# First MLP product as seven block products instead of eight, with its activations kept in DRAM

## The chip, the cores and the metric

The kernel runs on one core of a Trainium2 chip. The metric is device time in microseconds. A profile of one execution gives, for each engine (PE for matrix products, DVE for vector work, ACT for activations and copies, SP for issuing DMAs), when each instruction ran and what released it.

## The reference, cut to what matters

One layer of a diffusion block over 1024 latent tokens with 1024 features. Everything up to the MLP (norm, input projection, RG-LRU, Fourier mixing, merge, output projection) is the same before and after. The part that changes:

```python
def sq_relu_mlp(h, w1, w2):
    return jnp.square(jax.nn.relu(h @ w1)) @ w2

x = x + gt2 * sq_relu_mlp(modulate(rms_norm(x, g_mlp[i]), sh2, sc2), w1[i], w2[i])
return rms_norm(x, g_final)
```

Here `h` is 1024 tokens x 1024 features, `w1` is 1024 x 4096 and `w2` is 4096 x 1024, all in float32.

## The kernel before

Every float32 product is carried by three passes over an exact split x = hi + lo into the float32r type: hi\*hi + hi\*lo + lo\*hi. A split (`split`, L84) is a copy to hi on ACT and a subtraction to lo on DVE. A matmul instruction takes a 128 x 128 weight block and 512 columns.

Activations lie feature-major. Weights of `w1` come as 32 blocks of 128 output features; one block holds 8 slices of 128 input features. `Stream` (L94) loads such blocks three ahead into the four `wr` buffers (`wr_tile`, L78) and splits them two ahead into `wh` and `wl` (three buffers each).

Before the MLP, `out_mm` (L815) makes the output projection in two halves of 512 features (`dh`), eight token tiles each; a finished tile is added to `x2`, normalised by `norm_tile` (L795) into `xn`, and `norm_half` (L801) transposes four token tiles at a time, modulates them (scale and shift, on ACT or DVE) and splits them into `h2[h]`.

The MLP runs in eight chunks (`c`, L904) of four blocks (`f`). For each block `ff1` (L864) makes 2 token halves x 8 slices x 3 passes = 48 matmuls into a PSUM tile, `act` (L870) applies relu, squares and splits the result, and `load_w2` (L879) loads, scales by the gate and splits the matching rows of `w2`. Then `ff2` (L884) multiplies the chunk for eight token tiles, and DVE adds each result to `x2[i]` (L936). The products of one chunk and the vector work of the next overlap. After the last chunk the rows are normalised and stored.

What sets the order: outside of one early block, a planner orders the instructions of each engine by priority and by when it thinks that inputs are ready; `tc.high_priority(offset=...)` raises a priority by so many instructions. Inside `tc.manual_schedule` the instructions of the named engines keep the written order among themselves. All DMAs go through SP's one queue. Buffers come from tagged pools: `pg` has 24 of 1024 columns, `yp` 17, `wr` four; PSUM has three tiles of two banks (`mm_ps`) and two of one bank (`sm_ps`).

Of the kernel before, what the change touches and what calls it, by code (L numbers as in the profile page):

```python
"""Hybrid RG-LRU / Fourier diffusion block on one NeuronCore.

Activations are kept feature-major ([feature, token]); every float32 matrix product is
carried by three float32r passes over an exact split x = hi + lo (hi = float32r(x),
lo = x - hi, both exact in float32r): hi*hi + hi*lo + lo*hi.
"""
# [39 lines left out]
def f32(ap):  # L46
    return ap.bitcast(F32)
# [3 lines left out]
def block_kernel(es: ExitStack, tc: tile.TileContext, a, out):  # L51
# [13 lines left out]
    def nm(s):  # L65
        uid[0] += 1
        return f"{s}_{uid[0]}"
# [7 lines left out]
    def sm_ps():  # L75
        return psum.tile([P, HB], F32, tag="sm", name=nm("smp"), bufs=2)
# [17 lines left out]
    class Stream:  # L94
        """weight pages in the order of use: loads run three ahead, splits two ahead"""

# [38 lines left out]
    order += [(a["wlo"][m], W8) for m in range(KT)]  # L135
    order += [(a["w1"][f], W8) for f in range(FF // P)]
    weights = Stream(order)
# [3 lines left out]

# [1 line left out]
    ident = const.tile([P, P], F32, name="ident")  # L143
# [65 lines left out]
    gt_d = dram.tile([2, D], F32, name="gt_d")  # L209
    gyb_d = dram.tile([KT, P, T], F32, name="gyb_d")  # L210

    # persistent, small
    mod = const.tile([P, 64], F32, name="mod")
# [10 lines left out]
    def gemv_acc(wm, which, acc=None, ks=range(KT)):  # L224
        """silu(c) @ w_mod by rows, shift and scale of a pair of feature tiles"""
        if acc is None:
            acc = gacc[:, 4 * P * (nacc[0] % 2):4 * P * (nacc[0] % 2 + 1)]
            nacc[0] += 1
        for k in ks:
            sc = col(8 * which + k, silu)  # L230
            w = wm[k // 2][:, k % 2, :]
            if k == 0:
                V.tensor_scalar(acc, w, sc, None, ALU.mult)
            else:
                V.scalar_tensor_tensor(acc, w, sc, acc, ALU.mult, ALU.add)
        return acc

    def gemv_cols(kp, which, acc, ps=None):
        """columns of shift and (1 + scale) * g"""
        ps = sm_ps() if ps is None else ps  # L240
        for j in range(4):
            PE.matmul(ps[:, j:j + 1], acc[:, P * j:P * (j + 1)], ones, start=True, stop=True)
        b, kt = (M_SH1, M_SHC)[which] + 2 * kp, 2 * kp
        d = mod[:, b + 8:b + 10]
        V.tensor_tensor(mod[:, b:b + 2], ps[:, 0:4:2], pv[:, V_SH1 + kt:V_SH1 + kt + 2], ALU.add)
        V.tensor_tensor(d, ps[:, 1:4:2], pv[:, V_GMIX + kt:V_GMIX + kt + 2], ALU.mult)
        V.tensor_tensor(d, d, gb[:, kt:kt + 2], ALU.add)

    class Gemvs:
        """silu(c) @ w_mod for gates (rows, kept in DRAM) and the MLP's shift and scale, in steps"""  # L250

# [46 lines left out]

# [1 line left out]
    hT = [[page([P, T], F32R) for _ in range(2)] for _ in range(KT)]  # L300
# [16 lines left out]
    with tc.tile_pool(name="xp", bufs=16, reuse_waits="tile") as xp:  # L317
# [118 lines left out]

        # Fourier mixing, channels then positions, on the even/odd foldings of the inputs
        dcs = sm.tile([P, 130], F32, tag="dcs", name="dcs", bufs=1)
# [92 lines left out]
        ab += [page([P, 2, 2, NK], F32R) for _ in range(4)]  # L531
        # positions: rows are (group pair, channel frequency), columns the frequencies by parity
        pse = sm_ps()
# [35 lines left out]

# [1 line left out]
    prep_lam()  # L571
# [159 lines left out]

# [1 line left out]
    with tc.tile_pool(name="yp", bufs=17, reuse_waits="tile") as yp:  # L733
# [61 lines left out]
        def norm_tile(i):  # L795
            square_sum(x2[i], ss2[:, i:i + 1])
            r = rstd(ss2[:, i:i + 1])
            xn[i] = ypage([P, D])
            V.tensor_scalar(xn[i], x2[i], r, None, ALU.mult)

        def norm_half(h):  # L801
            for kt in range(KT):
                ps = sm_ps()
                for i in range(4):
                    PE.transpose(ps[:, i * P:(i + 1) * P], xn[4 * h + i][:, kt * P:(kt + 1) * P], ident)  # L805
                hf = sm.tile([P, HB], F32, tag="jk", name=nm("hf"), bufs=2)
                if kt % 2:
                    V.tensor_scalar(hf, ps, col(M_GS2 + kt, mod), col(M_SH2 + kt, mod), ALU.mult, ALU.add)
                else:
                    S.activation(hf, ps, AF.Identity, scale=col(M_GS2 + kt, mod), bias=col(M_SH2 + kt, mod))  # L810
                t = (page if h else ypage)([P, 2, HB], F32R)
                split(hf, t[:, 0], t[:, 1])
                h2[h][kt] = t

# [8 lines left out]
        for dh in range(2):  # L823
# [12 lines left out]
            for i in range(KT):  # L836
# [18 lines left out]
                if dh == 1:  # L855
                    norm_tile(i)
                    if i == 3:
                        norm_half(0)
        gv.reduce()
        norm_half(1)  # L860
        gt2 = const.tile([P, D], F32, tag="gt", name="gt2")
        dma(gt2, gt_d[1].partition_broadcast(P))

        def ff1(ps, w, h):  # L864
            for k in range(KT):
                for i, (l, r) in enumerate(passes(w, (h2[h][k][:, 0], h2[h][k][:, 1]))):
                    PE.matmul(ps[:, h * HB:(h + 1) * HB], l[:, k, :], r,  # L867
                              start=k == 0 and i == 0, stop=k == KT - 1 and i == 2)

        def act(ps):  # L870
            r = ypage([P, T])
            S.activation(r, ps, AF.Relu)
            hi, lo = ypage([P, T], F32R), ypage([P, T], F32R)
            S.activation(hi, r, AF.Square)  # L874
            V.tensor_tensor(r, r, r, ALU.mult)  # L875
            V.tensor_tensor(lo, r, f32(hi), ALU.subtract)
            return hi, lo
# [26 lines left out]
        for c in range(NC):  # L904
            av, wv = [], []
            if c == 0:
                ws, pss = [weights.take() for _ in range(3)], [mm_ps() for _ in range(3)]
                for h in range(2):
                    for w, ps in zip(ws, pss):
                        ff1(ps, w, h)  # L910
                for j, ps in enumerate(pss):
                    av.append(act(ps))
                    wv.append(load_w2(j))
            for f in range(len(av), CH):
                w, ps = weights.take(), mm_ps()
                for h in range(2):
                    ff1(ps, w, h)
                av.append(act(ps))
                wv.append(load_w2(c * CH + f))
            pss = [mm_ps() for _ in range(2)]  # L920
# [122 lines left out]
```

## Time and profile before

| what | value |
|---|---|
| runs shown, median (lowest to highest) | 1504.51 us (1504.46 to 1506.61) |
| span of the profiled execution, first to last instruction | 1501.4 us |
| PE busy | 1468.2 us, 98% of the span |
| DVE busy | 846.3 us, 56% |
| ACT busy | 536.6 us, 36% |
| DMA moved | 145.35 MB, mean 97 GB/s |

The page of the profile gives the execution's own time only as its span; a run's time has some 3 us beside it (1504.51 less 1501.4). Busy time counts the union of an engine's instructions; a matmul's shown duration overlaps the next one's, so what one costs is the distance between starts. In rows of instructions, "x24" means 24 merged ones, and a bracket gives the idle time before and what ended it.

### The profile page before, as it was taken

The numbers are of one execution on the slowest core, as the hardware profiler recorded it, in microseconds if no ns is written. First come the engines' busy times: TensorE is split into PE (matmuls) and PEld (weight loads), VectorE is DVE, ScalarE is ACT, GpSimd is POOL, SyncE is SP. The second block draws the span as 40 slices with busy tenths as digits, with TensorE's granted clock in tenths as the row PEclk, the third lists the DMA queues.
The fourth block names the chain that finished last, engine by engine and source line by source line (L and its number), as shares of the span: only waits on it lengthen the run. The fifth ranks groups of instructions, "written<-read, shape, count | busy, mean of one in ns | idle before, by whom it ended". The sixth has DMA issues, their size and how long they took to land.

```text
span 1501.4 us, 16062 instructions
## 1 busy us (share of the span) xinstructions
PE 1468.2 (98%) x6712; PEld 1193.8 (80%) x6712; DVE 846.3 (56%) x957; ACT 536.6 (36%) x643; POOL 0.7 (0%) x6
## 2 busy tenths in 40 slices
PE   5999999999999999999999999999999999999998
PEld 3888888878788877887778888888888888888886
DVE  7664649878987898556566343343424424343324
ACT  7443245765566647221254021120202113021122
POOL 0000000000000000000000000000000000000000
PEclk9999999999999999999999999999999999999999
DMA  8433612233313343559202020110202112020002
GB/s 329 175 112 119 237 39 81 101 124 133 110 61 128 115 150 126 182 177 339 73 29 98 14 85 28 56 56 28 72 14 71 42 43 66 5 85 28 28 1 112
DMA packets 42519, 145.35 MB, mean 97 GB/s; under 512 B 4755, under 2 KB 5163, under 8 KB 42447
## 3 DMA queue, kind: packets, MB, share of 16 engines
q1 hardware_dynamic: 42447, 144.34, 28.3%
q8 instruction: 52, 0.85, 0.2%
q14 instruction: 20, 0.16, 0.0%
HBM read 128.06 MB, written 16.26 MB: 96 GB/s over the span
## 4 chain that ended last, share of the span: by engine, by line
PE 89%; DVE 4%; DMA 2%; ACT 2%; issue 1%; SPq 0%; DVEq 0%; ACTq 0%
PE mm L867 24%; PE mm L889 23%; PE mm L307 23%; PE mm L819 6%; PE mm L762 5%; PE mm L607 2%; PE smp L582 2%; DMA wr<-in_win 1%; DVE l L639 1%; PE mm L483 1%; PE smp L608 1%; PE mm L672 1%; PE smp L805 1%; ACT jk L205 0%; DMA pg<-in_x 0%
## 5 line engine op out<-in xcount | busy, mean ns | idle before, releaser
L889 PE MATMUL mm<-pg,pg 128*128 128x512 f32 x1512 | 352.5, 394 | 0.0
L889 PEld LDWEIGHTS mm<-pg,pg 128*128 128x128 f32 x1512 | 283.8, 188 | 67.5
L867 PE MATMUL mm<-pg,wh 128*128 128x512 f32 x1024 | 323.1, 396 | 0.0
L307 PE MATMUL mm<-pg,wh 128*128 128x512 f32 x1120 | 308.7, 397 | 0.5 <-DVE pg L85 0.5
L307 PEld LDWEIGHTS mm<-pg,wh 128*128 128x128 f32 x1120 | 204.8, 189 | 43.8 <-DVE pg L85 1.0
L867 PEld LDWEIGHTS mm<-pg,wh 128*128 128x128 f32 x1024 | 191.9, 188 | 45.4
L85 ACT ACTIVATE wh<-wr 128x1024 fp32r<-128x1024 f32 (+2 forms) x92 | 91.3, 994 | 321.5 <-PE mm L867 161.1
L85 DVE TENSOR_TENSOR wl<-wr,wh 128x1024 fp32r<-128x1024 f32 (+2 forms) x92 | 104.8, 1141 | 172.9 <-ACT wh L85 172.9
L867 PE MATMUL mm<-pg,wl 128*128 128x512 f32 x512 | 201.8, 394 | 0.0
L85 ACT ACTIVATE pg<-wr 128x1024 fp32r<-128x1024 f32 (+1 forms) x55 | 51.2, 935 | 379.4 <-PE mm L889 262.6
L936 DVE TENSOR_TENSOR pg<-pg,mm 128x1024 f32<-128x1024 f32 x63 | 76.9, 1221 | 191.7 <-PE mm L889 191.7
L307 PE MATMUL mm<-pg,wl 128*128 128x512 f32 x560 | 175.4, 394 | 0.0
L307 PEld LDWEIGHTS mm<-pg,wl 128*128 128x128 f32 x560 | 105.4, 188 | 24.3
L867 PEld LDWEIGHTS mm<-pg,wl 128*128 128x128 f32 x512 | 96.2, 188 | 23.2
L819 PE MATMUL mm<-pg,pg 128*128 128x512 f32 x384 | 92.2, 397 | 0.1
L819 PEld LDWEIGHTS mm<-pg,pg 128*128 128x128 f32 x384 | 71.2, 188 | 18.2 <-DVE pg L85 1.2
L85 DVE TENSOR_TENSOR pg<-wr,pg 128x1024 fp32r<-128x1024 f32 (+1 forms) x55 | 58.3, 1067 | 25.9 <-ACT pg L85 25.9
L762 PE MATMUL mm<-pg,wh 128*128 128x512 f32 x256 | 70.1, 394 | 1.6 <-ACT pg L85 1.6
L875 DVE TENSOR_TENSOR pg<-pg 128x1024 f32<-128x1024 f32 x32 | 39.2, 1225 | 46.3 <-ACT pg L874 46.3
L762 PEld LDWEIGHTS mm<-pg,wh 128*128 128x128 f32 x256 | 47.9, 188 | 13.5 <-ACT pg L85 2.0
L205 ACT ACTIVATE jk<-pg 128x1024 bf16<-128x1024 f32 (+1 forms) x27 | 27.6, 1021 | 72.6 <-DVE pg L854 37.5
L747 DVE TENSOR_TENSOR wr<-wr,gt 128x1024 f32<-128x1024 f32 x32 | 39.2, 1225 | 24.4 <-DMA wr<-in_w 23.7
(216 smaller groups left out, 1496.3 us busy)
## 6 DMA issues: line engine op xcount, KB each, us to landing
wr<-in_w SPq DMA_DIRECT2D x64, 512.0 KB, 3.5
wr<-in_win SPq DMA_DIRECT2D x36, 512.0 KB, 4.5
pg<-in_wm SPq DMA_DIRECT2D x32, 512.0 KB, 7.8
wr<-in_wm SPq DMA_DIRECT2D x32, 512.0 KB, 3.7
pg<-in_x SPq DMA_DIRECT2D x16, 512.0 KB, 7.1
gyb_d<-l SPq DMA_DIRECT2D x8, 512.0 KB, 4.2
wr<-in_wlo SPq DMA_DIRECT2D x8, 512.0 KB, 4.3
wr<-ga_d SPq DMA_DIRECT2D x8, 512.0 KB, 4.2
```

What stands on the lines that cost most here:

```text
L85: return S.activation(hi, src, AF.Copy), V.tensor_tensor(lo, src, f32(hi), ALU.subtract)
L205: S.activation(j[:, 0:src.shape[1]], src, AF.Square, accum_out=dst)
L307: PE.matmul(ps[:, h * HB:(h + 1) * HB], l[:, k, :], r[:, h * HB:(h + 1) * HB], start=k == 0 and i == 0, stop=k == KT - 1 and i == 2)
L582: PE.matmul(pc[:, 0:TC], l[:, k, :], r[:, k % 4, :], start=k == 0 and i == 0, stop=k == KT - 1 and i == 2)
L607: PE.matmul(ps[:, h * HB:(h + 1) * HB], l, r[:, h * HB:(h + 1) * HB], start=i == 0, stop=i == 2)
L747: V.tensor_tensor(r, r, gate, ALU.mult)
L762: PE.matmul(ps[:, h * HB:(h + 1) * HB], l[:, k, :], r[:, h * HB:(h + 1) * HB], start=k == 0 and i == 0, stop=k == KT - 1 and i == 2)
L819: PE.matmul(ps, l, r, start=k == 0 and j == 0, stop=k == KT - 1 and j == 2)
L867: PE.matmul(ps[:, h * HB:(h + 1) * HB], l[:, k, :], r, start=k == 0 and i == 0, stop=k == KT - 1 and i == 2)
L875: V.tensor_tensor(r, r, r, ALU.mult)
L889: PE.matmul(ps[h], l, r[:, h * HB:(h + 1) * HB], start=f == 0 and j == 0, stop=f == CH - 1 and j == 2)
L936: V.tensor_tensor(x2[i], x2[i], pss[i], ALU.add)
```

## The change

The first MLP product, `w1` times `h`, is cut into 2 x 2 blocks: 16 pairs of feature blocks (a pair is 256 output features), two halves of the 1024 input features, two halves of the tokens. The block product is made by seven products with sums of blocks (Winograd's variant) instead of eight: with A the weights and B the activations, S1 to S4 are sums of weight blocks, T1 to T4 sums of activation blocks. Each product is 4 slices x 3 passes = 12 matmuls of 512 columns. Results that share terms are accumulated in the same PSUM bank, and DVE reads the bank between two products. The activations (relu, squared) are stored to `act_d` in DRAM, and `x2` to `x2_d`; both are loaded again for the second product. The two MLP products no longer alternate: first all 16 pairs, in a written order, then the eight chunks of `ff2`. The `Stream` no longer carries `w1`.

```diff
-    order += [(a["w1"][f], W8) for f in range(FF // P)]
...
+    x2_d = dram.tile([KT, P, D], F32, name="x2_d")
+    act_d = dram.tile([FF // P, P, T], F32, name="act_d")
...
+            dma(x2_d[i], x2[i])
+        def norm_block(kt, h, dst, on_vector):
+            ps = sm_ps()
+            for i in range(4):
+                PE.transpose(ps[:, i * P:(i + 1) * P], xn[4 * h + i][:, kt * P:(kt + 1) * P], ident)
+            if on_vector:
+                V.tensor_scalar(dst, ps, col(M_GS2 + kt, mod), col(M_SH2 + kt, mod), ALU.mult, ALU.add)
+            else:
+                S.activation(dst, ps, AF.Identity, scale=col(M_GS2 + kt, mod), bias=col(M_SH2 + kt, mod))
+        hf, tb = [], {n: [None] * 4 for n in ("b11", "b21", "b22", "t1", "t2", "t3", "t4")}
+        def norm_half0():
+            for k in range(4):
+                hf.append(page([P, 2, HB]))
+                for j in range(2):
+                    norm_block(k + 4 * j, 0, hf[k][:, j], j == 1)
+                    t = ypage([P, 2, HB], F32R)
+                    split(hf[k][:, j], t[:, 0], t[:, 1])
+                    tb[("b11", "b21")[j]][k] = (t[:, 0], t[:, 1])
+        def norm_half1(k):
+            g, t12, t34 = ypage([P, 2, HB]), *(wr_tile().rearrange("p (a b) -> p a b", b=HB) for _ in range(2))
+            for j in range(2):
+                norm_block(k + 4 * j, 1, g[:, j], False)
+            b11, b21, b12, b22 = hf[k][:, 0], hf[k][:, 1], g[:, 0], g[:, 1]
+            V.tensor_tensor(t12[:, 0], b12, b11, ALU.subtract)
+            V.tensor_tensor(t12[:, 1], b22, t12[:, 0], ALU.subtract)
+            V.tensor_tensor(t34[:, 0], b22, b12, ALU.subtract)
+            V.tensor_tensor(t34[:, 1], b21, t12[:, 1], ALU.subtract)
+            t = page([P, 2, HB], F32R)
+            split(b22, t[:, 0], t[:, 1])
+            tb["b22"][k] = (t[:, 0], t[:, 1])
+            for src, names in ((t12, ("t1", "t2")), (t34, ("t3", "t4"))):
+                hi, lo = page([P, 2, HB], F32R), page([P, 2, HB], F32R)
+                split(src, hi, lo)
+                for j, n in enumerate(names):
+                    tb[n][k] = (hi[:, j], lo[:, j])
...
-                        norm_half(0)
+                        norm_half0()
         gv.reduce()
-        norm_half(1)
...
+        class Pair:
+            def __init__(self, n):
+                self.n, self.w = n, {}
+            def load(self):
+                self.r = [wr_tile() for _ in range(2)]
+                for j, r in enumerate(self.r):
+                    dma(r, a["w1"][2 * self.n + j])
+            def put(self, src, names, hi, lo):
+                split(src, hi, lo)
+                for j, n in enumerate(names):
+                    self.w[n] = tuple(t[:, j * HB:(j + 1) * HB] for t in (hi, lo))
+            def hl(self, early=False):
+                if early:
+                    return ypage([P, 2 * HB], F32R), ypage([P, 2 * HB], F32R)
+                return tuple(wp.tile([P, 1024], F32R, tag=t, name=nm(t), bufs=3) for t in ("wh", "wl"))
+            def top(self, early=False):
+                self.put(self.r[0], ("a11", "a12"), *self.hl(early))
+            def sums13(self):
+                self.x = [ypage([P, 2 * HB]) for _ in range(2)]
+                (a11, a12), (a21, a22) = ([r[:, j * HB:(j + 1) * HB] for j in range(2)] for r in self.r)
+                self.q = a11, a12, a21, a22
+                V.tensor_tensor(self.x[0][:, 0:HB], a21, a22, ALU.add)
+                V.tensor_tensor(self.x[1][:, 0:HB], a11, a21, ALU.subtract)
+            def sums24(self):
+                a11, a12, a21, a22 = self.q
+                V.tensor_tensor(self.x[0][:, HB:], self.x[0][:, 0:HB], a11, ALU.subtract)
+                V.tensor_tensor(self.x[1][:, HB:], a12, self.x[0][:, HB:], ALU.subtract)
+            def s12(self):
+                self.put(self.x[0], ("s1", "s2"), *self.hl())
+            def s34(self):
+                self.put(self.x[1], ("s3", "s4"), *self.hl())
+            def last(self):
+                t = ypage([P, 2 * HB], F32R)
+                self.put(self.q[3], ("a22",), t[:, 0:HB], t[:, HB:])
+            def mm(self, ps, wn, tn, first):
+                for k in range(4):
+                    w = [t[:, k * P:(k + 1) * P] for t in self.w[wn]]
+                    for i, (l, r) in enumerate(passes(w, tb[tn][k])):
+                        PE.matmul(ps, l, r, start=first and k == 0 and i == 0, stop=k == 3 and i == 2,
+                                  skip_group_check=not first)
+            def p1(self):
+                ps = mm_ps()
+                self.A, self.B = ps[:, 0:HB], ps[:, HB:2 * HB]
+                self.e = (ypage if self.n else page)([P, 2 * HB])
+                self.mm(self.A, "a11", "b11", True)
+                S.activation(self.e[:, 0:HB], self.A, AF.Copy)
+            def p2(self):
+                self.f1 = page([P, T])
+                self.mm(self.A, "a12", "b21", False)
+                S.activation(self.f1[:, 0:HB], self.A, AF.Relu)
+            def p6(self):
+                self.mm(self.B, "s2", "t2", True)
+                V.tensor_tensor(self.e[:, HB:], self.e[:, 0:HB], self.B, ALU.add)
+            def p5(self):
+                self.C = sm_ps()
+                self.mm(self.C, "s1", "t1", True)
+            def p7(self):
+                self.f2 = page([P, T])
+                self.mm(self.B, "s3", "t3", False)
+                V.tensor_tensor(self.f2[:, HB:], self.e[:, 0:HB], self.B, ALU.add)
+                V.tensor_tensor(self.f2[:, HB:], self.f2[:, HB:], self.C, ALU.add)
+            def p3(self):
+                self.mm(self.C, "s4", "b22", False)
+                V.tensor_tensor(self.f1[:, HB:], self.e[:, HB:], self.C, ALU.add)
+                self.put_out(self.f1, 0)
+            def p4(self):
+                self.mm(self.B, "a22", "t4", False)
+            def out4(self):
+                V.tensor_tensor(self.f2[:, 0:HB], self.e[:, 0:HB], self.B, ALU.add)
+                self.put_out(self.f2, 1)
+            def put_out(self, t, j):
+                V.scalar_tensor_tensor(t, t, 0.0, t, ALU.max, ALU.mult)
+                dma(act_d[2 * self.n + j], t)
+        NP = FF // P // 2
+        pr = [Pair(n) for n in range(NP)]
+        with tc.high_priority(offset=PRIO):
+            pr[0].load()
+            pr[0].top()
+            pr[0].sums13()
+            pr[0].sums24()
+            pr[0].s12()
+            pr[0].s34()
+            pr[0].last()
+        with tc.manual_schedule(engines={mybir.EngineType.PE, mybir.EngineType.DVE, mybir.EngineType.Activation}):
+            pr[1].load()
+            pr[0].p1()
+            norm_half1(0)
+            pr[1].top(True)
+            pr[0].p2()
+            norm_half1(1)
+            pr[1].p1()
+            norm_half1(2)
+            pr[1].p2()
+            norm_half1(3)
+            pr[1].sums13()
+            pr[0].p6()
+            pr[1].sums24()
+            pr[1].s12()
+            pr[0].p5()
+            pr[2].load()
+            pr[0].p7()
+            pr[1].s34()
+            pr[1].last()
+            pr[0].p3()
+            pr[0].p4()
+            for n in range(1, NP):
+                c, nx = pr[n], pr[n + 1] if n + 1 < NP else None
+                if n > 1:
+                    c.p1()
+                pr[n - 1].out4()
+                if nx:
+                    nx.sums13()
+                c.p6()
+                if nx:
+                    nx.sums24()
+                c.p5()
+                if nx:
+                    nx.s12()
+                c.p7()
+                if n > 1:
+                    c.p2()
+                if nx:
+                    nx.top()
+                c.p3()
+                if nx:
+                    nx.s34()
+                    nx.last()
+                if n + 2 < NP:
+                    pr[n + 2].load()
+                c.p4()
+            pr[NP - 1].out4()
...
+        for i in range(KT):
+            x2[i] = page([P, D])
+            dma(x2[i], x2_d[i])
+        def load_act(f):
             hi, lo = ypage([P, T], F32R), ypage([P, T], F32R)
-            S.activation(hi, r, AF.Square)
-            V.tensor_tensor(r, r, r, ALU.mult)
-            V.tensor_tensor(lo, r, f32(hi), ALU.subtract)
+            load_split(act_d[f], hi, lo)
             return hi, lo
...
-            if c == 0:
-                ws, pss = [weights.take() for _ in range(3)], [mm_ps() for _ in range(3)]
-                for h in range(2):
-                    for w, ps in zip(ws, pss):
-                        ff1(ps, w, h)
-                for j, ps in enumerate(pss):
-                    av.append(act(ps))
-                    wv.append(load_w2(j))
-            for f in range(len(av), CH):
-                w, ps = weights.take(), mm_ps()
-                for h in range(2):
-                    ff1(ps, w, h)
-                av.append(act(ps))
-                wv.append(load_w2(c * CH + f))
+            for f in range(CH):
+                with tc.high_priority(offset=PRIO):
+                    av.append(load_act(c * CH + f))
+                    wv.append(load_w2(c * CH + f))
```

## Rows read from the trace of the kernel before

**Rows 1.** Page, parts 1 and 4: busy time, share, count; chain by engine and line.

```profile
PE 1468.2 (98%) x6712; PEld 1193.8 (80%) x6712; DVE 846.3 (56%) x957; ACT 536.6 (36%) x643; POOL 0.7 (0%) x6
...
PE mm L867 24%; PE mm L889 23%; PE mm L307 23%; PE mm L819 6%; PE mm L762 5%; PE mm L607 2%; PE smp L582 2%; DMA wr<-in_win 1%; DVE l L639 1%; PE mm L483 1%; PE smp L608 1%; PE mm L672 1%; PE smp L805 1%; ACT jk L205 0%; DMA pg<-in_x 0%
```

**Rows 2.** Stretches: us, busy PE, PEld, DVE, ACT, POOL, granted clock, DMA share, GB/s.

```profile
11.00:18.00 7.00, 2.00 (x5) 0.97 (x3) 6.79 (x15) 6.84 (x16) 0.00 (x0) 1.00 1.03 420
...
825.00:1450.00 625.00, 625.00 (x2689) 504.37 (x2688) 236.01 (x193) 112.77 (x110) 0.00 (x0) 1.00 0.14 43
```

**Rows 3.** Lines by form, 690 to 1500 us: count | busy us, mean ns | idle before.

```profile
L867 PE MATMUL mm<-pg,wh 128*128 128x512 f32 x1024 | 323.1, 396 | 0.0
L867 PE MATMUL mm<-pg,wl 128*128 128x512 f32 x512 | 201.8, 394 | 0.0
```

**Rows 4.** Same view, vector and activation forms that the new code uses.

```profile
L747 DVE TENSOR_TENSOR wr<-wr,gt 128x1024 f32<-128x1024 f32 x32 | 39.2, 1225 | 24.4 <-DMA wr<-in_w 23.7 <-DMA gt<-gt_d 0.2
L85 ACT ACTIVATE wh<-wr 128x1024 fp32r<-128x1024 f32 x29 | 30.8, 1060 | 161.1 <-PE mm L867 161.1
L853 DVE TENSOR_TENSOR g<-mm,gt 128x512 f32<-128x512 f32 x16 | 10.9, 687 | 22.5 <-PE mm L819 22.4
L898 DVE SCALAR_TENSOR_TENSOR pg<-pg,tiny,wr 128x1024 f32<-128x1024 f32 x7 | 9.0, 1284 | 0.2
L810 ACT ACTIVATE hf<-smp,mod 128x512 f32<-128x512 f32 x8 | 6.2, 777 | 3.4 <-PE smp L805 3.0 <-DVE pg L85 0.3
```

**Rows 5.** DVE in order of time: start, us; starts of neighbours show the pace.

```profile
710.16 1.29 DVE L853 TENSOR_TENSOR g<-mm,gt 128x512 f32<-128x512 f32 x2 [0.33 <-PE mm L819]
711.37 1.28 DVE L854 TENSOR_TENSOR pg<-pg,g 128x512 f32<-128x512 f32 x2
...
806.58 1.22 DVE L875 TENSOR_TENSOR pg<-pg 128x1024 f32<-128x1024 f32 x1
807.79 1.23 DVE L85 TENSOR_TENSOR pg<-wr,pg 128x1024 fp32r<-128x1024 f32 x1
808.93 1.22 DVE L876 TENSOR_TENSOR pg<-pg,pg 128x1024 fp32r<-128x1024 f32 x1
```

**Rows 6.** DVE in order of time, where the output projection ends.

```profile
776.42 1.42 DVE L799 TENSOR_SCALAR pg<-pg,tiny 128x1024 f32<-128x1024 f32 x2 [1.39 <-PE mm L819]
778.74 0.69 DVE L853 TENSOR_TENSOR g<-mm,gt 128x512 f32<-128x512 f32 x1 [0.90 <-PE mm L819]
...
781.90 0.75 DVE L799 TENSOR_SCALAR pg<-pg,tiny 128x1024 f32<-128x1024 f32 x1
```

**Rows 7.** PE in order of time, same place.

```profile
772.97 5.73 PE L819 MATMUL mm<-pg,pg 128*128 128x512 f32 x24
778.54 0.60 PE L805 MATMUL smp<-ident,pg 128*128 128x128 f32 x4
```

**Rows 8.** SP's queue in order of time: start, us, line, what is loaded.

```profile
602.36 0.32 SPq L705 DMA_DIRECT2D gyb_d<-l  x1
603.51 0.32 SPq L768 DMA_DIRECT2D wr<-gyb_d  x1
...
641.84 7.97 SPq L745 DMA_DIRECT2D wr<-in_w_out  x2
650.62 0.33 SPq L113 DMA_DIRECT2D wr<-in_w  x1
```

**Rows 9.** DVE in the early block with a written order (loop over kt).

```profile
47.01 1.53 DVE L235 SCALAR_TENSOR_TENSOR gacc<-pg,silu,gacc 128x512 f32<-128x512 f32 x2
48.49 0.29 DVE L85 TENSOR_TENSOR dcl<-dcs,dch 128x130 fp32r<-128x130 f32 x1
48.70 1.53 DVE L235 SCALAR_TENSOR_TENSOR gacc<-pg,silu,gacc 128x512 f32<-128x512 f32 x2
```

**Rows 10.** PE in order of time, first products after the sparse start.

```profile
32.32 1.11 PE L367 MATMUL smp<-ident,pg 128*128 128x128 f32 x4 [0.21 <-ACT pg L374]
33.09 2.05 PE L307 MATMUL mm<-pg,wh 128*128 128x512 f32 x4
34.94 1.05 PE L307 MATMUL mm<-pg,wl 128*128 128x512 f32 x2
35.79 1.53 PE L307 MATMUL mm<-pg,wh 128*128 128x512 f32 x4
37.15 0.63 PE L307 MATMUL mm<-pg,wl 128*128 128x512 f32 x2
```

**Rows 11.** Page, part 6: DMA issues, KB each, median us from issue to landing.

```profile
wr<-in_w SPq DMA_DIRECT2D x64, 512.0 KB, 3.5
...
gyb_d<-l SPq DMA_DIRECT2D x8, 512.0 KB, 4.2
```

More of the change, by code (lines that the diff above doesn't have):

```diff
@@ L799, in norm_tile @@
             V.tensor_scalar(xn[i], x2[i], r, None, ALU.mult)
[L801 to L813, printed above, removed]
+            dma(x2_d[i], x2[i])
@@ L857, in block_kernel @@
                     if i == 3:
-                        norm_half(0)
+                        norm_half0()
         gv.reduce()
-        norm_half(1)
         gt2 = const.tile([P, D], F32, tag="gt", name="gt2")
         dma(gt2, gt_d[1].partition_broadcast(P))
[L864 to L868, printed above, removed]
@@ L870, in act @@
-        def act(ps):
-            r = ypage([P, T])
-            S.activation(r, ps, AF.Relu)
+        class Pair:
[71 more added lines that the diff above has]
+                dma(act_d[2 * self.n + j], t)
```

## Prediction

> **What bounds the kernel now.** I read the page's busy shares and chain first, then stretches, then lines, then DVE, PE and SP in order of time. PE is busy for 98% of the span and the chain of waits lies on it, 24% of the span on the first MLP product (L867) and 23% on the second (L889) [rows 1]. From 825 to 1450 us PE starts 2689 products in 625.00 us without a gap, 0.2324 us each, while DVE works 236 us and ACT 113 [rows 2]. The reader should not take the 396 ns of one matmul for its cost: neighbours overlap, so the distance of starts counts. L867 has 1024 + 512 = 1536 matmuls and no idle time in front of them [rows 3]. So fewer matmuls are worth their full time here, as long as PE still finds its inputs.
>
> **What goes.** Per pair of feature blocks 96 matmuls become 7 x 12 = 84. Over 16 pairs 192 go: 192 x 0.2324 = 44.6 us. The transposes (64) and the w1 loads (32) stay. With `act` go an ACT relu and square and two DVE operations per block, which PE hid already; nothing is gained by them.
>
> **A pair in the middle.** PE needs 84 x 0.2324 = 19.5 us. On DVE, subtractions of 512 columns follow each other every 0.60 us (0.73 where one needs the other's result), those of 1024 every 1.14, and one that reads PSUM is no longer than one that doesn't, 687 ns [rows 4, 5]. Per pair: four sums 2.6 us, three splits of 1024 and one of 512 columns 4.0, five additions from PSUM 3.4, two squares of 1.2 (1284 ns each alone) 2.4; together 12.4 of 19.5. ACT: three copies of 1060 ns and three of 512 columns, estimated at 0.6 each from that, 5.0 us. The risk is in the order, not in the sum. Bank B is written by p6, read by DVE, and written again by p7; C is read after p7 and written by p3; B again before p4. I followed the written order, 2.8 us for each product: p6 ends 5.6 us into a pair, its read ends at 6.4, p7 starts at 8.4 (p5 lies between); p7's two reads end at 12.6, p3 starts at 13.9 (p2 lies between). The `wh`/`wl` buffers of the next pair come free one product ahead of their copies, and each split is ready a product or more before PE asks for it: the tops at 16.9 of 19.5, s34 and `last` 1.2 us into the next pair, where p7 wants them at 8.4. So PE waits for nothing in pairs 2 to 15; bounds 0 and 0.9 us a pair (were two operations of 1.14 us to fall in front of p7's reads, these would end at 14.8, where p3 could start at 13.9). I take 0, the value that the written order gives. Pair 1 has no p2 between p7 and p3, since its p2 was done earlier: there p3 waits for the two reads, 1.4 us.
>
> **Where the stage starts.** In the trace the last output product ends at 778.70 (772.97 + 5.73) [rows 7]; its normalised tile is written at 782.65, 4.0 us later [rows 6]. Only then can the second token half be transposed, and now four rounds of `norm_half1` follow, on whose T blocks p6, p5 and p7 wait. DVE per round: four subtractions 2.6 us, splits of 512 + 1024 + 1024 columns 2.9; 5.5 us, four rounds 22.0. Pair 1's `top` stands between them, 1.1. Pair 0's sums and splits (2.6 + 2.3 + 0.6 = 5.5) are raised in priority, but I expect no head start for them. Buffers of one pool seem to be given out in the order of the code whatever the priority: the first w1 load, raised by 600, was issued at 650.62, behind two w_out loads that come before it in the code [rows 8]. Pair 0's sums are written to `yp` buffers, which come after `xn[7]`; and `xn[5]` and `xn[6]` already wait for buffers until the last product runs (776.42, released by L819) [rows 6]. So DVE has 5.5 + 22.0 + 1.1 = 28.6 us to do from +4.0, to +32.6; the T2 that p6 waits for is ready 1.1 sooner, +31.5. Then PE: the last three matmuls of p6 0.7, p5 and p7 5.6, the two reads of 1.4 before p3, p3 and p4 5.6: +44.8. What PE has to do meanwhile is 9 products, 25.1 us, and 32 transposes, four in 0.60 [rows 7], 4.8: 29.9. **Stall 14.9 us.** Bounds: 9.4, if pair 0 is prepared beforehand after all; 21.1, if DVE also sits idle in each round for ACT's two modulations (2 x 0.777 [rows 4], four times 6.2). Before, PE had no gap here. I take 14.9 because rows 6 and 8 both speak for the order of buffers.
>
> **PE's clock.** After the sparse first 33 us the first ten matmuls of L307 take from 33.09 to 37.15, 4.06 us in place of 2.32: 1.7 us lost, although the granted clock reads 1.00 in such stretches too; 0.46 us each is the pace of the lower level, 1.2 GHz, and 0.2324 fits the upper, 2.4 GHz [rows 2, 10]. In the start of the stage PE is idle for a few us at p1 of pair 1 and longer in p6. I take one such loss, 1.7; bounds 0 and 3.5.
>
> The Trainium skill, in "TensorE: Matmul & The Clock Gate" (Part 1: The HAM clock gate), says that the throttled clock is the resting state and only activity lifts it. By that rule both idle times, not just the longer one, would cost a slow restart, and the sum would come out 1.7 us higher. The slow first products of the trace agree with the rule; whether gaps of some us suffice no row here shows.
>
> **Where the second product starts.** The first chunk needs activations and w2, loaded, scaled and split, and `x2` back. Instructions from outside can slip into a written order: the `dcl` split ran at 48.49 in the middle of the early block's loop [rows 9]. And a load from DRAM waits only for its own part: gyb_d's first row was loaded 1.15 us after its last was issued for storing, sooner than the 4.2 us a store takes to land [rows 8, 11]. So three blocks of activations can be split during the last pair, when DVE has no next pair to prepare. w2 comes later: in the order of the code `x2`'s eight buffers precede it, they fit after p5 and are asked for after p2, 5.6 us before PE is done; two w2 blocks follow by p3's end and a third soon after. The fourth stands behind 4.2 MB of `x2`, 10 us at the 420 GB/s that one stretch shows [rows 2]: landed 5.7 us after p4, scaled (1.2) and split (1.1 + 1.2) at 9.2, where PE wants it after 36 matmuls, 8.4. With something for the first block, 2.0 us. Bounds: 0, and 11.4 if none of it slips ahead (load 3.5 [rows 11], last outputs 2.0, first block 3.5, and the next three each 0.8 slower than PE's 2.8).
>
> **Also added, hidden.** 64 DRAM transfers for activations and 16 for `x2`, 42 MB. Per pair 1 MB in and 1 MB out in 19.5 us, 108 GB/s, against 420 seen. SP is in order, so a store that waits for DVE holds up the loads behind it; w1 of pair n + 2 is asked for a whole pair before its first sum, 20 us against 3.5 to land. In the second product DVE has eight splits, four scalings and eight additions of 1024 columns per chunk, 20 x 1.2 = 24 us of PE's 44.6.
>
> **Sum.** -44.6 + 14.9 + 1.4 + 1.7 + 2.0 = -24.6 us. On the profiled span 1501.4 - 24.6 = 1476.8. A run's time has 3.1 us beside the span (median 1504.51), which the change doesn't touch: 1479.9, say **1480 us**.
>
> **Rivals.**
> - *The start is prepared ahead.* Pair 0's sums are made before `xn[7]`, no clock loss, no wait at the second product: 1480 - 5.5 - 1.7 - 2.0 = 1471. For it: DVE has gaps up to 778 us [rows 6]; against it: the buffers.
> - *The border between the products lies open.* Nothing of the first chunk is ready when p4 ends: 1480 - 2.0 + 11.4 = 1489. For it: w2's buffers come free last; against it: rows 9.
> - *Every bank that is used twice makes PE wait (slower).* If DVE runs behind by more than the product in between, p7 and p3 each wait out their reads: 0.69 + 1.42 = 2.1 us a pair, and up to 4.4 with a 1.14 us operation in front of each; over 15 pairs 32 to 66 us: 1512 to 1546, I take 1512. From 24.6 / 15 = 1.6 us a pair on the change loses. For it: DVE's order is fixed, its queue holds ACT's copies in the chain (`top` waits for p2's relu), and slack at p3 is only 1.3 us. Against it: 12.4 of 19.5 us of load.
>
> The Trainium skill speaks for that last rival: "Perfetto Trace Analysis" (Matmuls) wants independent groups of matmuls to rotate through PSUM banks, so that one bank is read while another is written. This change goes back to a bank just read three times a pair; by the rule, unmet, the time is the 1512 above. No row of before shows such a reuse.
>
> **Chances.** Forecast 0.50, start ahead 0.16, open border 0.20, banks 0.14 (of which 0.04 lands about level). A difference under 0.2%, 3 us, can't be told from no change. The first three are faster: 0.86; same 0.04; slower 0.10. The range runs from 1467 (start ahead, with the tail below it) to 1494 (open border and some of the 21.1 us start); it leaves out the banks and the far ends.
>
> **What would show it.** L867's successor has 1344 matmuls at 0.232 us, and the middle pairs repeat every 19.5 us with no PE idle; a period above 21 is the bank rival. Idle PE of 12 to 18 us lies between the last output product and p4 of pair 0, ended by DVE's lo of the T blocks, with pair 0's sums after the last `xn`. A few matmuls after it start 0.4 us or more apart. At the border PE waits under 4 us, for w2's fourth block. The forecast is wrong if the start costs under 9 or over 21 us, or if pairs are longer than 19.8.

## The result and the profile after

The changed kernel takes **1518.8 us** (median of 4 runs, 1515.4 to 1520.4) against 1504.5 before (4 runs, 1504.3 to 1506.6): ratio 1.0091, 95% interval 1.0076 to 1.0105. It is slower, where 1480 was forecast, and the time lies outside the range. The profiled execution took 1515.4, its span is 1513.6, 12.2 more than before. It is the fastest of the four, 3.4 us below their median; so a difference of medians against this kernel can be larger by that than the one between two profiles, and stages are best compared by profiles.

The page after, parts 1 and 4, answering to [rows 1]:

```profile
PE 1440.4 (95%) x6520; PEld 1161.8 (77%) x6520; DVE 973.4 (64%) x1149; ACT 553.5 (37%) x683; POOL 0.7 (0%) x6
...
PE 84%; DVE 7%; ACT 4%; DMA 3%; issue 2%; SPq 0%; DVEq 0%; ACTq 0%
```

PE has the 192 instructions fewer that were promised and 27.8 us less busy time, yet its share falls from 98% to 95%: it now waits. The stretches (columns as in [rows 2]) show where:

```profile
780.00:790.00 10.00, 4.08 (x20) 2.70 (x18) 10.00 (x13) 8.20 (x11) 0.00 (x0) 0.87 0.32 107
790.00:800.00 10.00, 10.00 (x43) 8.17 (x44) 9.29 (x13) 7.56 (x11) 0.00 (x0) 0.78 0.00 0
800.00:810.00 10.00, 5.88 (x16) 4.11 (x16) 9.86 (x14) 4.88 (x7) 0.00 (x0) 0.73 0.31 95
...
840.00:1080.00 240.00, 223.18 (x936) 173.53 (x935) 138.81 (x168) 53.27 (x67) 0.00 (x0) 1.00 0.29 101
...
1160.00:1170.00 10.00, 5.89 (x16) 4.31 (x15) 9.91 (x10) 5.01 (x6) 0.00 (x0) 0.66 0.78 252
...
1180.00:1480.00 300.00, 300.00 (x1294) 242.67 (x1293) 148.12 (x128) 50.18 (x53) 0.00 (x0) 1.00 0.25 83
```

There are three places: the start (780 to 820), the border (1140 to 1170), and all the time between. From 840 to 1080 PE starts 936 matmuls in 240 us, 0.256 us each, where [rows 2] have 0.2324; in the second product (last row) the old pace is back. DVE is busy for 139 of these 240 us, so it is not the bound. The list of PE's waits, from 760 us to the end (what waited, for whom: us in total, times, longest):

```profile
PE mm L940 <- DVE pg L966: 11.1, 14, 1.0
PE mm L940 <- ACT pg L948: 9.6, 14, 0.7
PE mm L940 <- ACT pg L85: 7.9, 2, 5.2
PE mm L1064 <- DVE pg L1101: 4.1, 1, 4.1
PE smp L940 <- DVE pg L967: 3.0, 2, 1.5
PE mm L1064 <- DVE pg L85: 3.0, 1, 3.0
PE mm L940 <- DVE pg L85: 2.1, 2, 1.4
```

Read the counts first: two waits come 14 times, once in each of pairs 2 to 15. L940 is the matmul of a pair, L948 ACT's copy of bank A after p1, L966 DVE's read of bank B after p7. One pair in PE's order of time:

```profile
861.64 0.40 PE L940 MATMUL mm<-pg,wl 128*128 128x512 f32 x1
862.73 0.73 PE L940 MATMUL mm<-pg,wh 128*128 128x512 f32 x2 [0.69 <-ACT pg L948]
863.29 0.40 PE L940 MATMUL mm<-pg,wl 128*128 128x512 f32 x1
...
868.39 0.63 PE L940 MATMUL mm<-pg,wh 128*128 128x512 f32 x2
...
870.95 0.40 PE L940 MATMUL mm<-pg,wl 128*128 128x512 f32 x1
872.12 0.73 PE L940 MATMUL mm<-pg,wh 128*128 128x512 f32 x2 [0.78 <-DVE pg L966]
872.70 0.40 PE L940 MATMUL mm<-pg,wl 128*128 128x512 f32 x1
...
884.25 0.73 PE L940 MATMUL mm<-pg,wh 128*128 128x512 f32 x2 [0.69 <-ACT pg L948]
```

p6 starts at 862.73 and again at 884.25: the pair repeats every 21.52 us, not 19.52. At 862.73 p6 begins to write bank **B**, and waits for the copy of bank **A**. At 872.12 p2 begins to write **A**, and waits for the read of **B**. At 868.39 p7 goes back to B itself, which DVE has just read, and waits for nothing. A wait takes more than the idle time beside it: from 861.64 to 863.29 three matmuls start in 1.65 us instead of 0.70, 0.95 lost for 0.69 shown; at p2 it is 1.05 for 0.78. Together 2.0 us a pair.

Neither wait is needed by the data. A and B are the two 512-column halves of one tile (`self.A, self.B = ps[:, 0:HB], ps[:, HB:2 * HB]`). The theory to test: the program waits for the last reader of the whole tile, not of the half that is written.

### The profile page after: what moved, and what is told of

Same layout as the page of the kernel before. It is cut to its first block, busy times and chain, and to the rows that moved or that the text cites. A ratio compares the mean times of both kernels' runs of the same rounds, so it can differ in the third digit from the quotient of the medians.

```text
span 1513.6 us, 16235 instructions
## 1 busy us (share of the span) xinstructions
PE 1440.4 (95%) x6520; PEld 1161.8 (77%) x6520; DVE 973.4 (64%) x1149; ACT 553.5 (37%) x683; POOL 0.7 (0%) x6
## 4 chain that ended last, share of the span: by engine, by line
PE 84%; DVE 7%; ACT 4%; DMA 3%; issue 2%; SPq 0%; DVEq 0%; ACTq 0%
PE mm L1064 22%; PE mm L308 22%; PE mm L940 14%; PE mm L847 6%; PE smp L940 6%; PE mm L763 6%; PE mm L608 2%; PE smp L583 1%; DMA wr<-in_win 1%; DMA wr<-act_d 1%; DVE pg L85 1%; DVE l L640 1%; DVE pg L966 1%; ACT jk L204 1%; PE mm L484 1%
## 5 line engine op out<-in xcount | busy, mean ns | idle before, releaser
L1064 PE MATMUL mm<-pg,pg 128*128 128x512 f32 x1512 | 355.5, 397 | 7.1 <-DVE pg L1101 4.1
L308 PE MATMUL mm<-pg,wh 128*128 128x512 f32 x1120 | 308.5, 397 | 0.5 <-DVE pg L85 0.5
L308 PEld LDWEIGHTS mm<-pg,wh 128*128 128x128 f32 x1120 | 204.7, 189 | 43.7 <-DVE pg L85 1.0
L85 ACT ACTIVATE pg<-wr 128x1024 fp32r<-128x1024 f32 (+1 forms) x112 | 101.1, 931 | 278.3 <-PE mm L1064 175.7
L940 PE MATMUL mm<-pg,wh 128*128 128x512 f32 x496 | 159.5, 402 | 24.9 <-DVE pg L966 11.1
L308 PE MATMUL mm<-pg,wl 128*128 128x512 f32 x560 | 175.4, 394 | 0.0
L940 PEld LDWEIGHTS mm<-pg,wh 128*128 128x128 f32 x496 | 90.8, 188 | 58.0 <-DVE pg L966 17.3
L85 DVE TENSOR_TENSOR pg<-wr,pg 128x1024 fp32r<-128x1024 f32 (+1 forms) x112 | 116.6, 1067 | 27.3 <-ACT pg L85 27.1
L308 PEld LDWEIGHTS mm<-pg,wl 128*128 128x128 f32 x560 | 105.4, 188 | 24.3
L940 PE MATMUL mm<-pg,wl 128*128 128x512 f32 x248 | 98.2, 396 | 0.0
L847 PE MATMUL mm<-pg,pg 128*128 128x512 f32 x384 | 91.9, 397 | 0.0
L940 PE MATMUL smp<-pg,wh 128*128 128x512 f32 x256 | 82.0, 402 | 3.0 <-DVE pg L967 3.0
L85 ACT ACTIVATE wh<-pg 128x1024 fp32r<-128x1024 f32 x32 | 33.9, 1063 | 113.6 <-PE smp L940 94.9
L763 PE MATMUL mm<-pg,wh 128*128 128x512 f32 x256 | 70.0, 394 | 1.6 <-ACT pg L85 1.6
L940 PE MATMUL mm<-pg,pg 128*128 128x512 f32 x216 | 55.9, 408 | 5.9 <-ACT pg L85 5.2
L940 PEld LDWEIGHTS smp<-pg,wh 128*128 128x128 f32 x256 | 49.0, 192 | 15.5 <-DVE pg L967 3.9
```

Source lines behind the costliest of these rows:

```text
L85: return S.activation(hi, src, AF.Copy), V.tensor_tensor(lo, src, f32(hi), ALU.subtract)
L308: PE.matmul(ps[:, h * HB:(h + 1) * HB], l[:, k, :], r[:, h * HB:(h + 1) * HB], start=k == 0 and i == 0, stop=k == KT - 1 and i == 2)
L763: PE.matmul(ps[:, h * HB:(h + 1) * HB], l[:, k, :], r[:, h * HB:(h + 1) * HB], start=k == 0 and i == 0, stop=k == KT - 1 and i == 2)
L847: PE.matmul(ps, l, r, start=k == 0 and j == 0, stop=k == KT - 1 and j == 2)
L940: PE.matmul(ps, l, r, start=first and k == 0 and i == 0, stop=k == 3 and i == 2, skip_group_check=not first)
L1064: PE.matmul(ps[h], l, r[:, h * HB:(h + 1) * HB], start=f == 0 and j == 0, stop=f == CH - 1 and j == 2)
```

## The experiments

The kernels differ from the changed one by the diff shown. "Before" ran beside each group, at 1503.2 to 1504.5 us.

**Two tiles.**

```
-                self.A, self.B = ps[:, 0:HB], ps[:, HB:2 * HB]
+                self.A = ps[:, 0:HB]
             def p6(self):
+                self.B = mm_ps()[:, 0:HB]
```

> Banks A and B of a pair come from two tiles of `mm_ps` instead of the two halves of one; every operation, its engine and its place in the order stay. Theory (a wait goes by tile, not by half: p6 on B waits for ACT's copy of A, p2 on A for DVE's read of B): the pair shrinks from 21.5 to 19.5 us, both waits are gone from the chain of the middle pairs, time 1518.8 - 14 x 2.0 = about 1491 us. Rival 1 (a bank that is used twice makes PE wait for the reads of that same bank): a separate tile changes nothing, 1518 us and 21.5 us a pair. Rival 2 (DVE and ACT run late for the pair): the waits move to p7 and p3, 1510 to 1518 us.

Measured 1487.4 us, ratio to before 0.9883 (0.9868 to 0.9898): 31.4 less than the changed kernel. In its stretches PE starts as many matmuls in 240 us as it did before, 0.2323 us each, and DVE has done more in the time:

```profile
840.00:1080.00 240.00, 240.00 (x1033) 193.66 (x1032) 154.26 (x187) 58.10 (x73) 0.00 (x0) 1.00 0.32 109
```

p4 of pair 1 ends at 837.38, the second product starts at 1111.37: 274.0 / 14 = 19.57 us a pair, against (1139.09 - 837.69) / 14 = 21.53. The pairs give 27.4 us; the medians differ by 31.4, the two profiled executions by 27.9. Rivals 1 and 2 fall: every bank is still written, read and written again, DVE's order is the same, and PE waits for neither.

**The counter-test: C beside A.** Two tiles also bring more banks into rotation, so the same theory was made to produce a loss in another place.

```
-                self.A, self.B = ps[:, 0:HB], ps[:, HB:2 * HB]
+                self.A, self.C = ps[:, 0:HB], ps[:, HB:2 * HB]
             def p6(self):
+                self.B = mm_ps()[:, 0:HB]
             def p5(self):
-                self.C = sm_ps()
```

> The counter-test to the two tiles (1487.4 us): B keeps its tile, but now C takes the second half of A's tile, in place of a buffer of its own. No operation more or less. Theory (a wait goes by tile): p2 on A now waits for DVE's read of C after p7 (L967 as the second of two reads, about 1.4 us and a restart), p3 on C for ACT's relu of A (0.7 us): 2.1 us in the records and 2.5 to 3 us a pair, period about 22.3 us, times 14 = 35 to 42 us: 1522 to 1530 us. Rival 1 (the two tiles won because more banks rotate, three in place of two): one bank less than in the kernel with two tiles but still more than in the changed kernel, 1487 to 1500 us. Rival 2 (waits go by bank): 1487 us.

Measured 1527.3 us, ratio 1.0152 (1.0136 to 1.0167), within what the theory gave; the period is 22.45 us. PE's waits from 838 to 1150 us are the two foretold, p2 on A for the read of C, p3 on C for the relu of A:

```profile
PE mm L940 <- DVE pg L967: 21.7, 14, 2.2
PE mm L940 <- ACT pg L953: 9.6, 14, 0.7
```

This kernel takes as many `mm_ps` tiles a pair as the last one and is 40 us slower. It takes four banks a pair, the changed kernel three, and is 8.5 us slower than that one too: banks in rotation don't explain the gain. That waits go by tile is shown from both sides.

**One wait of the two.**

```
-                S.activation(self.e[:, 0:HB], self.A, AF.Copy)
+                S.activation(self.e[:, 0:HB], gt2[:, 0:HB] if self.n > 1 else self.A, AF.Copy)
```

> The changed kernel, but from pair 2 on ACT's copy (L948) reads a constant page of the same size in place of bank A, so that the product of p1 is left out of the sums. Everything else stays, A and B in one tile. Theory (two waits by tile, each with its own price): p6 no longer waits for ACT, p2 still waits for DVE's read of B (L966); the period goes from 21.5 to 20.5 us, 14 x 1.0 = 14 us: about 1504 us. Rival (a single bound sets the period, the waits only share it): what p6 doesn't wait, p2 does, 1517 to 1519 us.

From pair 2 on this kernel leaves the product of p1 out of the sums, so only its time is of use. Measured 1501.1 us, ratio 0.9989 (0.9979 to 0.9999): 17.7 less (15.9 between the profiled executions), 14 were expected. The period is (1123.97 - 836.21) / 14 = 20.55, so this wait cost 0.98 us a pair, or 13.7; the other stays as it was:

```profile
PE mm L940 <- DVE pg L966: 10.9, 14, 0.8
```

The waits add up; no common bound hides behind them.

**The start.** Only pair 0's sums get other buffers:

```
-                self.x = [ypage([P, 2 * HB]) for _ in range(2)]
+                self.x = [(ypage if self.n else page)([P, 2 * HB]) for _ in range(2)]
```

> Only the buffers of pair 0's sums are other ones (pool `page` instead of `yp`), so that they no longer stand behind the last `xn` in the order in which buffers are given out. Theory (pair 0's sums ran after xn[7] for want of a buffer, and the four rounds of `norm_half1` stood behind them): sums L918 to L924 run before 777, the stall between the last output product and p4 of pair 0 falls from 17.7 to about 12 us, time about 1513 us. Rival (DVE's four rounds alone set the end, since PE's waits lie on each round's transposes): 1517 to 1519 us.

Measured 1514.9 us, ratio 1.0067 (1.0051 to 1.0084): 3.9 less. DVE of the changed kernel, then of this one (L800 writes a normalised tile, L918 to L924 are the sums):

```profile
777.39 0.75 DVE L800 TENSOR_SCALAR pg<-pg,tiny 128x1024 f32<-128x1024 f32 x1
778.06 0.68 DVE L918 TENSOR_TENSOR pg<-wr 128x512 f32<-128x512 f32 x1
```

```profile
765.90 0.68 DVE L918 TENSOR_TENSOR pg<-wr 128x512 f32<-128x512 f32 x1
...
773.02 0.68 DVE L924 TENSOR_TENSOR pg<-wr,pg 128x512 f32<-128x512 f32 x1
...
781.16 0.75 DVE L800 TENSOR_SCALAR pg<-pg,tiny 128x1024 f32<-128x1024 f32 x1
```

The sums follow the last tile in the one and run ahead of it in the other. From the end of the last output product to the end of p4(0) it is 43.8 us (777.49 to 821.27) in place of 47.8. Of these 4.0 us, 1.2 are three matmuls that followed that product and now stand ahead of it (two of L283, 0.95 us, and one of L940, 0.23); some 2.8 are stall that is gone. The want of a buffer had kept the sums back, as the forecast had it; of the 5.5 us that it allowed for them about half came. Between the two profiled executions only 0.6 us is left of the gain, since this one came to the stage's first transposes 2.2 us later (743.18, against 740.98) and waits for 5.88 us instead of 4.11 at the border.

**The border, by priority.**

```
-                with tc.high_priority(offset=PRIO):
+                with tc.high_priority(offset=PRIO if c == 0 else 0):
```

> Only the loads and splits of the second product's first chunk are raised in priority; those of chunk 1 go by the order of the code, behind the first chunk's products and the addition of `x2`. Theory (the addition of tile 0's `x2` is ready at about 1155 but DVE, in order, runs it at 1163.5, behind chunk 1's splits that wait for loads): the wait of 4.1 us in front of L1064 at 1164.8 goes, and with it the slow clock that follows, 1512 to 1515 us, pairs unchanged at 21.5. Rival (the bank's release isn't the cause, the loads themselves are late): the wait stays or moves to chunk 1's first products, 1517 to 1522 us.

Measured 1511.4 us (5 runs, 1509.2 to 1514.2), ratio 1.0042 (1.0027 to 1.0056). The reason given fails in its trace, which is of the slowest of the five runs: the addition has moved forward in DVE's order, but the wait for it is still there. That the time lies next to the 1512 to 1515 expected is no support for that reason.

```profile
1143.05 16.51 PE L1064 MATMUL mm<-pg,pg 128*128 128x512 f32 x70 [3.18 <-DVE pg L85]
1163.64 11.53 PE L1064 MATMUL mm<-pg,pg 128*128 128x512 f32 x39 [4.08 <-DVE pg L1101]
```

What the other runs gained is not shown by a profile and stays open. The changed kernel has the same two waits, in its PE rows:

```profile
1139.09 0.63 PE L1064 MATMUL mm<-pg,pg 128*128 128x512 f32 x2
1142.71 17.95 PE L1064 MATMUL mm<-pg,pg 128*128 128x512 f32 x70 [2.99 <-DVE pg L85]
1164.77 15.52 PE L1064 MATMUL mm<-pg,pg 128*128 128x512 f32 x56 [4.11 <-DVE pg L1101]
```

There, SP's queue and then ACT, in order of time, lead to the cause:

```profile
1138.54 0.32 SPq L983 DMA_DIRECT2D act_d<-pg  x1
1138.91 1.19 SPq L1047 DMA_DIRECT2D pg<-x_d  x2
1141.55 0.32 SPq L983 DMA_DIRECT2D act_d<-pg  x1
1141.91 2.75 SPq L1047 DMA_DIRECT2D pg<-x_d  x4
1144.76 0.41 SPq L746 DMA_DIRECT2D wr<-act_d  x1
```

```profile
1153.13 1.06 ACT L85 ACTIVATE pg<-wr 128x1024 fp32r<-128x1024 f32 x1 [12.32 <-DMA wr<-act_d]
```

`x2`'s last four loads stand behind the last store of activations, which waits for DVE, and the fourth block of activations stands behind them. ACT gets it at 1153.13, 14.0 us after the second product's first matmul. DVE stands idle for it for 8.17 us, and the addition that PE waits for comes behind the splits:

```profile
1154.23 1.23 DVE L85 TENSOR_TENSOR pg<-wr,pg 128x1024 fp32r<-128x1024 f32 x1 [8.17 <-ACT pg L85]
...
1163.50 1.21 DVE L1101 TENSOR_TENSOR pg<-pg,mm 128x1024 f32<-128x1024 f32 x1
```

PE doesn't wait for the fourth block itself. Its first 2 + 70 matmuls are three token tiles of 24 each, as many as there are `mm_ps` tiles; the fourth token tile needs the first addition, which frees one.

**`x2` later, alone.**

```
-        for i in range(KT):
-            x2[i] = page([P, D])
-            dma(x2[i], x2_d[i])
...
                     wv.append(load_w2(c * CH + f))
+            if c == 0:
+                for i in range(KT):
+                    x2[i] = page([P, D])
+                    dma(x2[i], x2_d[i])
```

> The changed kernel with one edit: `x2` is reloaded after the first chunk's loads in the order of the code; A and B stay in one tile, priorities stay. In the trace of the changed kernel the second product takes 368.2 us from its first matmul to its last, in the kernel with x2 later 355.6. Theory (the border costs those 12.6 us, and x2's place in the order of buffers and queues is the cause): 368.2 falls to about 356, pairs stay at 21.5, time 1518.8 - 12.6 = about 1506 us. Rival (the raised priority of chunk 1's loads holds up the additions of x2 by itself): the wait for L1101 stays, 1510 to 1514 us.

Measured 1503.7 us, ratio 0.9997 (0.9987 to 1.0006): 15.1 less (11.5 between the profiled executions), level with the eight products. The second product runs without a wait from its first matmul,

```profile
1139.26 35.94 PE L1060 MATMUL mm<-pg,pg 128*128 128x512 f32 x155
```

and takes 356.5 us (1139.26 to 1495.74) in place of 368.2. `x2`'s place is the cause; whether its buffers or its traffic weigh more isn't separated, since the edit moves both. The rival that gave priority the blame falls: it was left as it was.

**The three edits together** (two tiles, priority, pair 0's buffers).

> All three edits together. Theory: 1518.8 - 28 - 5 - 5 = about 1480 us, faster than the kernel with eight products (1504.5) by 1.6%; pairs of 19.5 us. Rival (what one edit gives is taken back by the next wait): between 1491 and 1505 us, no better than the two tiles alone.

Measured 1480.3 us, ratio 0.9834 (0.9819 to 0.9849), as the theory gave; the rival falls.

**The three and `x2` later.**

> The three edits together (1480.3 us) and, beside them, `x2` reloaded after the first chunk's loads in the order of the code, not before them. Theory (the first chunk's w2 splits wait for pages that stand behind x2's eight, and the fourth block's activations land behind x2's 4 MB, 10 us after they were asked for): the first wait of L1065 for DVE's L85, 3.8 us, falls below 1, the activations of block 3 are split before PE asks, no half-rate products: 1473 to 1476 us. Rival (DVE is simply late there, behind the last pair's sums): under 1 us of difference, 1479 to 1481. Other rival: x2 now comes late for its own additions and PE waits for a bank, 1480 to 1486.

Measured 1473.7 us (median of three; a run of 2864 us, whose cause isn't known, is left out), ratio 0.9801 (0.9784 to 0.9817). The second product takes 355.6 us (1111.68 to 1467.24), 6.9 less than with the three edits, and has no wait at all.

**Pair 1's first split ahead of the written order.**

```
+            pr[1].load()
+            pr[1].top(True)
         with tc.manual_schedule(engines={mybir.EngineType.PE, mybir.EngineType.DVE, mybir.EngineType.Activation}):
-            pr[1].load()
             pr[0].p1()
             norm_half1(0)
-            pr[1].top(True)
```

> As the kernel with x2 later, and pair 1's load and first split stand before the written order in place of in its first round. Theory (in the start every microsecond of DVE between the last output product and p6 is paid for by PE): 1.1 us less than that kernel. Rival (`yp` buffers are given out in the order of the code, so the T blocks now wait behind the split's two buffers): no gain, or up to 3 us more.

Measured **1471.0 us**, ratio 0.9783 (0.9767 to 0.9800), the fastest here. From the last output product to p4(0) it is 42.1 us against 44.0, 1.9 less, not 1.1: with its weights split, p1 of pair 1 runs at 784.49 already, inside DVE's first round. The rest of the 2.7 is within the scatter of these runs.

## Why the prediction was wrong, by its own steps

| step | forecast, us | measured, us |
|---|---|---|
| 192 matmuls gone | -44.6 | -44.6 (6712 to 6520) |
| start, with the clock | 14.9 + 1.7 = +16.6 | 47.8 - 29.9 = +17.9 |
| pair 1 | +1.4 | 837.69 - 821.96 - 60 x 0.2324 = +1.8 |
| pairs 2 to 15 | 0 | 301.4 - 14 x 19.52 = **+28.1** |
| second product's start | +2.0 | 368.2 - 355.6 = **+12.6** |
| sum | -24.6 | +15.8; the span shows +12.2 |

The 3.6 us between the sum and the span belong to no step. The last output product ends at 774.20, 4.5 sooner than in [rows 7]. For 1.1 of this the execution was that much ahead already at the stage's first transposes (740.98, before 742.09). For 3.1, work that before ran ahead of this product now follows it (769.88 to 772.97 in the trace of before: two matmuls of L282, two transposes and the first eight of L867). The two of L282, L283 in the changed kernel, lie inside the 47.8 and make 0.95 of the 17.9 us; they have only moved. The 3.1 us that the prediction adds beside the span are 1.8 in the changed kernel.

**The middle pairs: the step that failed.** "So PE waits for nothing in pairs 2 to 15", with 0.9 us a pair as the upper bound. The order, the durations and DVE's load that it was read from all came true: DVE's reads take 687 ns each, 139 of 240 us are busy, p7 and p3 start without a wait from pair 2 on. What was never asked is what a wait is tied to. The text took each of A, B and C for itself, while the diff took one tile for A and B. p6 then stands right behind p1 and its copy, and p2 right behind p7 and its read, and the written order lets no other product slip in between: 2 x 1.0 us a pair. One part of the rival fits, 2.1 us a pair for two reads waited out, and its time of 1512 was nearer than the forecast; its mechanism was wrong, since the banks used twice cost nothing. The rule of the Trainium skill that spoke for it ("Perfetto Trace Analysis", Matmuls) has groups of matmuls rotate through banks. The runs here agree that a read beside another group's matmuls is what one wants, but B is reused after one product in between without a wait, and it was the second half of a tile that made one.

**The second product's start: the late block was right, its price was not.** The forecast had the fourth block behind `x2`, landing 5.7 us after p4, and PE waiting for it, under 4 us. It reached ACT after 14.0, since `x2`'s loads share SP's queue with the last stores and half of them were issued only at 1141.91, after p4 had ended. PE waited 7.1 us, and for other things: 2.99 for a split of the first block, since only two matmuls had run, and 4.11 for the addition that frees a PSUM tile and that DVE, in order, made only behind the late splits, a path that the forecast doesn't have. Both waits were followed by slow matmuls, 70 in 17.95 us and 56 in 15.52, which is 1.7 and 2.5 more than 0.2324 each.

**The start: right.** Sum and cause held, the split didn't: recorded waits make 11.5 of the 17.9 and slow matmuls most of the remainder, and the longer wait lies at p1 of pair 1, not in p6. DVE is busy for 29.15 of the 30 us from 780 to 810. That fits a chain on DVE that sets the end, in which a product that runs slowly only shortens the next wait; no run tries this by itself.

```profile
768.36 5.84 PE L847 MATMUL mm<-pg,pg 128*128 128x512 f32 x24
...
787.93 1.22 PE L940 MATMUL mm<-pg,pg 128*128 128x512 f32 x2 [5.17 <-ACT pg L85]
789.90 4.59 PE L940 MATMUL mm<-pg,pg 128*128 128x512 f32 x10 [0.75 <-DVE pg L85]
794.33 1.04 PE L807 MATMUL smp<-ident,pg 128*128 128x128 f32 x8
...
803.93 0.50 PE L940 MATMUL mm<-pg,wh 128*128 128x512 f32 x1 [2.77 <-ACT pg L85]
805.78 0.79 PE L940 MATMUL mm<-pg,wh 128*128 128x512 f32 x1 [1.35 <-DVE pg L85]
...
816.12 0.73 PE L940 MATMUL smp<-pg,wh 128*128 128x512 f32 x2 [1.50 <-DVE pg L967]
819.02 2.94 PE L940 MATMUL mm<-pg,pg 128*128 128x512 f32 x12
```

The reader sees PE of the changed kernel from the last output product to p4(0), which ends at 821.96. After the waits of 5.17 and 0.75 us ten matmuls take 4.43 us from the first start to that of the next row, 0.44 each, nearly twice the usual distance; the last row has twelve, done in 2.94.

**Hidden, as forecast:** the added traffic. From 840 to 1080 us it is 101 GB/s (108 worked out), and no wait of PE there leads to a DMA.

## What to carry to other kernels

Before a written order is priced, ask of every buffer what a wait on it is tied to: two banks that are halves of one tile behaved as one here, and an order written out by hand keeps PE from filling the gap. One microsecond in a loop of 14 pairs weighs more than a stall of ten at its edge, so check the steady state first, by the distance of two like rows. Where a stage ends, write down the order of its queues (SP's here): a reload that is wanted late but asked for early delays what is wanted first.

## What the runs showed of the hardware

A wait of PE costs more than its recorded idle time: 0.95 and 1.05 us for 0.69 and 0.78, and 0.98 when one of them was taken away. The rows of one pair show where the rest lies. The idle time counts from the shown end of a matmul, 0.40 us after its start, where the next one would have started after 0.23; that is 0.17 us. And from the first two matmuls after the wait to the next start it is 0.56 us (862.73 to 863.29), in place of 0.46; that is 0.1.

The granted clock did show the slow matmuls here: 0.87, 0.78 and 0.73 from 780 to 810 us, where waits of 5.17 and 2.77 us lie, and 0.66 from 1160 to 1170, with one of 4.11 us. The 0.44 us of the ten matmuls is close to the 0.46 of [rows 10], the pace of the lower level, 1.2 GHz. In [rows 10] the clock couldn't show it: the clock records in the trace of before begin 36.7 us into the span, so the 1.00 that the view prints for earlier stretches is no reading, and the prediction was wrong to take it for one. The idle times of 0.7 to 1.0 us twice a pair left the granted clock at 1.00 all the way from 840 to 1080, and so did the 1.50 us in front of p3 in pair 1. How long a wait was does not decide it alone: at the border of the changed kernel one of 2.99 us was followed by 70 matmuls in 17.95 us, in the kernel of the border by priority one of 3.18 us by 70 in 16.51, 0.236 each. The resting state that the Trainium skill gives the clock ("TensorE: Matmul & The Clock Gate", Part 1) agrees with the slow products after the waits above; that both idle times of the start would be followed by a slow stretch came true, and the first stretch alone cost 4.43 - 10 x 0.2324 = 2.1 us, more than the 1.7 that the prediction gave for one.
